# A one-core mixer and mixture-of-experts kernel: expert weights read in longer pieces, the scatter matmuls in one run, final_g by one transfer

## The chip, the cores and the metric

One Trainium2 chip, one of its cores. The time is device microseconds of one execution of the whole program; lower is better. A kernel's time is the median of several executions.

## The reference, cut to what matters

```python
def reference(x, ln1_g, ..., w_out, ln2_g, ..., w_exp_gate, w_exp_up, w_exp_down, final_g):
    ...
    for l in range(DEPTH):                                   # DEPTH = 1
        x = mixer_sublayer(x, ln1_g[l], w_in[l], ..., w_out[l])
        x = x + hier_moe(rmsnorm(x, ln2_g[l]), ...)
    return rmsnorm(x, final_g)

def hier_moe(h, w_rg, b_rg, w_re, b_re, w_gate, w_up, w_down):
    t = h.reshape(-1, d)                                     # 256 tokens x 1024
    ...                                                      # best group of 4, then its best 2 of 4 experts
    combine = jnp.sum(jax.nn.one_hot(expert_ids, N_EXPERTS, dtype=f32) * w_sel[..., None], axis=1)
    y = jnp.zeros((n, d), f32)
    for e in range(N_EXPERTS):                               # 16 experts, 512 channels inside
        a = jax.nn.silu(t @ w_gate[e]) * (t @ w_up[e])
        y = y + combine[:, e:e + 1] * (a @ w_down[e]).astype(f32)
    return ...
```

Everything is float32. The three expert weights hold 16 x 1024 x 512 numbers each, 2 MB per expert and matrix.

## The kernel before, in words

The program is one function. Its first part (up to 200 us) is the mixer: the projections of w_in, stick-breaking attention and the HGRN2 recurrence. Then come the projection by w_out with the routing, and the experts.

**What lies where.** x2 holds the 256 tokens as 2 tiles of 128 tokens (t = 0, 1) by 1024 channels. After the mixer it is split into xH (a copy rounded to the matmul's fp32r type, by ACT) and xL (the rest, by POOL), both in o_hl (lines 674 to 676), in plain channel order. A channel sits in the expert tiles at block k of 128 and partition p: channel 128k+p. The gain ln2_g is laid out to match by vectors() (line 266): a transpose of small rows into the columns `cols`, of which g2c is a part.

**Routing.** As each 256-channel quarter of w_out's product comes out of PE (o_mm), DVE adds it to x2 (o_add, line 668), ACT squares it for the norm (o_sq), PE transposes it (o_tr), DVE copies the transposes to SBUF (line 660) and PE multiplies them by the router weights (o_lg, line 664, into plg). route_rank (line 720) ranks the 20 logits by all-pair comparisons on DVE (ceq, cgt: lines 727 to 730); route_pos (line 736) numbers each expert's tokens with two small matmuls (prk) and makes posm; onehot (line 694) writes, for 4 experts and 64 rows each, the matrix Sr (in the buffer mr) that picks tokens. A function residual(i) adds a quarter of x to the output sum py[i] with two matmuls by the identity (line 830; moving operands xH and xL).

**Gather.** gather(q) collects for two pairs of experts the chosen tokens' rows, transposed: 32 matmuls with 128 channels of xH or xL as stationary operand and Sr as moving operand (line 928, tile pg; line 750 for the first), and ACT or DVE multiplies the result by g2c into xg.

**Expert pairs.** 16 experts are done as 8 pairs p = 0..7. For each pair PE does, in program order:

- gateup(p, "g"): 32 matmuls into pg (line 958), then gateup(p, "u"): 32 into pu. Each is 64 rows by 512 columns; the two experts j = 0, 1 of a pair alternate.
- scatter(p-1): 8 matmuls (line 992) add the previous pair's result yh to py. Four of them stand between the 16th and the 17th matmul of pu, four behind the 32nd.
- mid(p): ACT and DVE make silu(gate) times up in abuf, PE transposes it in 4 blocks (pT, line 967), DVE copies that to the buffer mf (line 968).
- for odd p the next gather; then prep(p+1): small matmuls into the tile pw (lines 943, 945), DVE copies two columns (cwall, lines 947, 948), ACT copies pw to STa in the buffer mr (line 949; listed in the trace as `ACT L60 mr<-pw`, since the helper at line 60 issues it).
- down(p): the columns in two halves, 16 matmuls into one PSUM tile pd and then 16 into the next (line 977); after each half weigh (line 981) scales it on ACT and DVE into yh.

The PSUM tiles pw, pT, pg of the gathers and pd share two tags, C0 and B0, in turn:

```python
911:     def wtile():
912:         wtile.n += 1
913:         return ("C0", "B0")[wtile.n % 2]
```

so a tile can be written only when the tile two places before it has been read out.

**Weights.** Every pair needs 12 tiles of 1 MB: gate and up of both experts in two halves of 512 channels, down in two column halves. SP issues their DMAs in the order of use, each as soon as one of a ring of 1 MB slots comes free. A transfer takes for each partition 4 rows that lie 128 rows apart in DRAM:

```python
880:                     wts[nm, p, j, kh] = load(
881:                         w[2 * p + j].rearrange("(k p) f -> p k f", p=P)[:, 4 * kh:4 * kh + 4], [4, DE],
```

that is 4 pieces of 2048 bytes (512 columns of 4 bytes). The last pair's down tiles are cut further.

**The end.** load_gain and bcast_gain (lines 997 to 1008) bring final_g as one row and spread it over 128 partitions with 4 matmuls (tile pgf) and two ACT copies, ahead of the last pair's pu. After the last pair's down the sum py is normalised and stored.

The order of PE's instructions is that of the program; a scheduler puts the other engines' instructions in order by readiness and priority, unless the code forces it.

Of the kernel before, what the change touches and what calls it, by code (L numbers as in the profile page):

```python
# [30 lines left out]
def hybrid_kernel(ctx: ExitStack, tc: tile.TileContext, x, ln1_g, w_in, w_bsb, w_bhg, hg_norm_g,  # L31
# [48 lines left out]
    rowt = blk("w0", [2, P], name="rowt")  # L80
# [4 lines left out]
    nc.scalar.dma_start(rows[12:20], ln2_g.rearrange("(k p) -> k p", p=P))  # L85

# [60 lines left out]
    cols = cp.tile([P, 20], F32, name="cols")  # L147
# [520 lines left out]
    def o_add(t, c0, c1, pp):  # L668
        V.tensor_add(x2[:, t, c0:c1], x2[:, t, c0:c1], pp)

    def o_sq(i, t, c0, c1):
        act(xL[:, t, c0:c1], x2[:, t, c0:c1], AF.Square, accum_out=ss2[:, t, i:i + 1])

    def o_hl(t, c0, c1):
        act(xH[:, t, c0:c1], x2[:, t, c0:c1], AF.Copy)
        nc.gpsimd.tensor_sub(xL[:, t, c0:c1], x2[:, t, c0:c1], xH[:, t, c0:c1].bitcast(F32))

    def o_ev(i, t, c0, c1, pp):
        o_add(t, c0, c1, pp)
        o_sq(i, t, c0, c1)  # L680
        o_hl(t, c0, c1)
# [38 lines left out]
    def route_rank(t):  # L720

        l5, c, e = lg[:, t], cgt[:, t], ceq[:, t]
        V.scalar_tensor_tensor(l5.rearrange("p g e -> p (g e)"), plg[:, t, 0:20], sc[:, t:t + 1], br,
                               ALU.mult, ALU.add)
# [11 lines left out]
    def route_pos(t):  # L736
# [8 lines left out]
        V.scalar_tensor_tensor(posm[:, t], prk[:, t], 1.0, self_[:, t], ALU.add, ALU.mult)  # L745

    def gather0(t):
        for k in range(KT):
# [28 lines left out]
    with tc.high_priority():  # L777
# [12 lines left out]
            (6, 3): [(o_lg, 2, 0), (o_tr, 3, 0)], (7, 0): [(o_lg, 3, 0), (route_rank, 0)],  # L790
            (7, 1): [(o_tr, 0, 1)], (7, 2): [(o_lg, 0, 1), (o_tr, 1, 1)], (7, 3): [(o_lg, 1, 1), (route_pos, 0)]}
    for n in (6, 7):
# [4 lines left out]
        if n == 6:  # L797
            o_ev(0, 1, 0, 512, pq[0, 1])
    mr = blk("yha", [4, 256], F32R, name="mr")
# [5 lines left out]
    with tc.high_priority():  # L805
        o_add(1, 512, 768, pq[1, 1][:, 0:256])
        o_sq(1, 1, 512, 768)
    o_tr(2, 1, "D1", late[0])
    with tc.high_priority():
        o_add(1, 768, 1024, pq[1, 1][:, 256:512])  # L810
        o_sq(2, 1, 768, 1024)
        V.tensor_add(ss2[:, 1, 0:1], ss2[:, 1, 0:1], ss2[:, 1, 1:2])
        route_pre(1)
    o_tr(3, 1, "B0", late[1])
    route_rms(1, 2, ss2[:, 1, 2:3])
    onehot(0, 0)
    o_hl(1, 512, 768)
    o_hl(1, 768, 1024)
    o_lg(2, 1, late[0])
    o_lg(3, 1, late[1])  # L820
    pgs = [ps.tile([P, 2, 256], F32, name="pg0_%d" % k2, tag=["A0", "A1", "C0", "B0"][k2]) for k2 in range(4)]
# [4 lines left out]
    def residual(i):  # L826
        t, dh = divmod(i, 2)
        py[i] = ps.tile([P, 512], F32, name="py_%d" % i, tag=PYT[i])
        for j, xx in enumerate((xH, xL)):
            nc.tensor.matmul(py[i], idr, xx[:, t, 512 * dh:512 * dh + 512],  # L830
                             start=j == 0, stop=False, skip_group_check=True)

    gather0(0)
    residual(0)
    route_rank(1)
    residual(1)
    route_pos(1)
    onehot(0, 1)
    residual(2)
# [45 lines left out]
    def load_d(p):  # L885
        for dh in range(2):
            src = [w_down[2 * p + j].rearrange("(k p) d -> p k d", p=P)[:, :, 512 * dh:512 * dh + 512]
                   for j in range(2)]
            cut = p == NP - 1
            for j in range(2):  # L890
                wts["d", p, j, dh] = load(src[j], [4, 512], parts=2 if cut else 1)
            if not cut:
                pieces = ()
            elif dh == 0:
                pieces = ((0, 2, 0, 512), (2, 4, 0, 512))
            else:
# [19 lines left out]
    def gather(q):  # L916
# [4 lines left out]
        for k2 in range(KT // 2):  # L921
# [10 lines left out]
            if k2 % 2:  # L932
                V.tensor_tensor(xg[:, ks], pg, g2c[:, ks, None].to_broadcast([P, 2, 256]), ALU.mult)
            else:
                for j in range(2):
                    k = 2 * k2 + j
                    act(xg[:, k], pg[:, j], AF.Copy, scale=g2c[:, k:k + 1])
# [13 lines left out]
    def gateup(p, nm, between=None):  # L951
        pt = ps.tile([P, DE], F32, name="p%s%d" % (nm, p), tag="A0" if nm == "g" else "A1")
        xg = xgs[p // 2][:, :, (p % 2) * P:(p % 2) * P + P]
        for k in range(KT):
            if k == KT // 2 and between:
                between()
# [5 lines left out]
    def mid(p, pgt, put):  # L962
# [3 lines left out]
        for f in range(4):  # L966
            nc.tensor.transpose(pT[:, f], abuf[:, f * P:f * P + P], ident)
        V.tensor_copy(aT_, pT)

    def down(p, c0, c1, between=None):  # L970
        pd = ps.tile([P, c1 - c0], F32, name="pd%d_%d" % (p, c0), tag=wtile())
        dh, o = c0 // 512, c0 // 512 * 512
        for f in range(4):
            if f == 2 and between:
                between()
            for j in range(2):
                nc.tensor.matmul(pd[j * 64:j * 64 + 64], aT_[:, f, j * 64:j * 64 + 64],  # L977
                                 wts["d", p, j, dh][:, f, c0 - o:c1 - o], start=f == 0, stop=f == 3)
        return pd

# [200 lines left out]
```

## Time and profile before

| | us |
|---|---|
| median of 3 runs | 459.32 (458.93 to 461.73) |
| the profiled execution's own time | 461.8 |
| its span on the core | 460.1 |
| PE busy in the span | 439.5 (96%) |
| mean granted TensorE clock in the span | 0.984 of full |

In the views PE is TensorE's matmuls, DVE VectorE, ACT ScalarE, POOL GpSimd, SP SyncE (it issues the DMAs). A tile's name is the program's, with numbers left out: wt a weight tile, pg, pu, pd and py the PSUM tiles above. "Idle before" is how long the engine stood still ahead of an instruction, with the engine that released it.

### The profile page before, as it was taken

The page shows a single profiled execution, that of the slowest core. Times are in us where ns is not written, and L with a number is a line of the kernel's source. Part 1 is how long each engine was busy: PE and PEld are TensorE (multiplying, and loading weights), DVE is VectorE, ACT ScalarE, POOL GpSimd, SP SyncE. Part 2 cuts the span into 40 slices and gives each one's busy share as a digit, 9 for nine tenths or more (in the row PEclk, how much of TensorE's full clock was granted, in tenths as well). Part 3 has the DMA queues.
Part 4 walks back from the last instruction along what each step waited for, and adds up shares of the span by engine and source line. Part 5 has one row for each costly group of instructions (what it writes and reads, how often), then busy time and mean ns, then how long its engine had stood idle before and what let it go on. Part 6 is the DMA issues. An engine that isn't in the chain of part 4 may idle for free.

```text
span 460.1 us, 6095 instructions
## 1 busy us (share of the span) xinstructions
PE 439.5 (96%) x2429; PEld 286.5 (62%) x2429; DVE 193.6 (42%) x315; ACT 149.4 (32%) x246; POOL 103.0 (22%) x121
## 2 busy tenths in 40 slices
PE   6999999999999999999998999999999999999991
PEld 6999899887777888878743345343633336343350
DVE  5878857595546647974722112020210203011032
ACT  6644335535656745523311102101110102101223
POOL 8464755675144200352200000000000000000000
PEclk9999999999999999999799999999999999999996
DMA  8945342525939999568959999999999999999952
GB/s 290 289 157 181 112 166 93 182 93 150 389 118 358 292 386 385 178 233 280 341 185 388 387 387 386 387 386 387 387 386 387 386 387 385 387 387 385 386 193 98
DMA packets 73852, 134.79 MB, mean 293 GB/s; under 512 B 2317, under 2 KB 14665, under 8 KB 73818
## 3 DMA queue, kind: packets, MB, share of 16 engines
q1 hardware_dynamic: 73634, 134.23, 81.7%
q8 instruction: 21, 0.34, 0.3%
q0 software_dynamic: 128, 0.09, 0.2%
q14 instruction: 13, 0.11, 0.1%
q10 hardware_dynamic: 56, 0.01, 0.0%
HBM read 133.28 MB, written 1.05 MB: 292 GB/s over the span
## 4 chain that ended last, share of the span: by engine, by line
PE 85%; DMA 4%; POOL 4%; DVE 2%; issue 2%; ACT 1%; POOLq 0%; ACTq 0%
PE pu L958 12%; PE pg L958 11%; PE pd L977 11%; PE pv L294 5%; PE pv L295 5%; PE pv L296 5%; PE py L992 4%; PE pp L200 3%; DMA wt<-in_w_exp_gate_dram 3%; PE pp L201 3%; PE pp L202 3%; PE pg L928 3%; PE pl L365 2%; PE pp L309 1%; PE pb L601 1%
## 5 line engine op out<-in xcount | busy, mean ns | idle before, releaser
L191 DVE TENSOR_TENSOR lp<-wt,hp 128x1024 fp32r<-128x1024 f32 (+1 forms) x43 | 59.6, 1405 | 23.0 <-ACT hp L60 22.6
L977 PE MATMUL pd<-wt,mf 128*64 128x512 f32 (+1 forms) x272 | 57.2, 571 | 2.6 <-ACT mr L60 1.4
L958 PE MATMUL pu<-wt,xg 128*64 128x512 f32 x256 | 58.6, 596 | 0.0
L958 PE MATMUL pg<-wt,xg 128*64 128x512 f32 x256 | 57.4, 593 | 0.5 <-DMA wt<-in_w_exp_gate_dram 0.5
L60 ACT ACTIVATE hp<-wt 128x1024 fp32r<-128x1024 f32 (+1 forms) x44 | 44.6, 1036 | 40.2 <-PE pp L201 26.7
L704 POOL TENSOR_SCALAR rb<-ss,rb 128x1 f32<-128x1 f32 x1 | 0.5, 527 | 226.2 <-ACT junk L60 226.2
L964 DVE SCALAR_TENSOR_TENSOR mf<-pu,cwall,mf 128x512 f32<-128x512 f32 x8 | 6.0, 752 | 106.1 <-PE pu L958 106.1
L958 PEld LDWEIGHTS pg<-wt,xg 128*64 128x64 f32 x256 | 18.9, 137 | 37.0 <-issue 35.2
L200 PE MATMUL pp<-hTH,hp 128*128 128x256 f32 x144 | 41.4, 287 | 0.0
L977 PEld LDWEIGHTS pd<-wt,mf 128*64 128x64 f32 x272 | 19.5, 137 | 34.9 <-issue 30.7
L201 PE MATMUL pp<-hTL,hp 128*128 128x256 f32 x144 | 40.7, 283 | 0.0
L202 PE MATMUL pp<-hTH,lp 128*128 128x256 f32 x144 | 40.7, 283 | 0.0
L958 PEld LDWEIGHTS pu<-wt,xg 128*64 128x64 f32 x256 | 18.6, 137 | 34.5 <-issue 33.3
L294 PE MATMUL pv<-hp,hTH 128*128 128x512 f32 x96 | 39.7, 414 | 0.0
L295 PE MATMUL pv<-lp,hTH 128*128 128x512 f32 x96 | 37.5, 391 | 0.0
L296 PE MATMUL pv<-hp,hTL 128*128 128x512 f32 x96 | 37.5, 391 | 0.0
L983 DVE SCALAR_TENSOR_TENSOR yh<-pd,cwall,yh 128x512 fp32r<-128x512 f32 (+1 forms) x16 | 11.7, 734 | 48.8 <-ACT yh L60 48.8
L60 ACT ACTIVATE yh<-pd,cwall 128x512 fp32r<-128x512 f32 (+1 forms) x16 | 10.8, 674 | 54.8 <-PE pd L977 54.8
L200 PEld LDWEIGHTS pp<-hTH,hp 128*128 128x128 f32 x144 | 27.6, 191 | 0.2
L201 PEld LDWEIGHTS pp<-hTL,hp 128*128 128x128 f32 x144 | 27.6, 192 | 0.0
L202 PEld LDWEIGHTS pp<-hTH,lp 128*128 128x128 f32 x144 | 27.6, 192 | 0.0
L294 PEld LDWEIGHTS pv<-hp,hTH 128*128 128x128 f32 x96 | 18.0, 188 | 5.0 <-issue 0.8
(277 smaller groups left out, 720.5 us busy)
## 6 DMA issues: line engine op xcount, KB each, us to landing
wt<-in_w_exp_gate_dram SPq DMA_DIRECT2D x32, 1024.0 KB, 13.7
wt<-in_w_exp_up_dram SPq DMA_DIRECT2D x32, 1024.0 KB, 13.9
wt<-in_w_exp_down_dram SPq DMA_DIRECT2D x28, 1024.0 KB, 14.1
wt<-in_w_in_dram SPq DMA_DIRECT2D x22, 1024.0 KB, 6.2
wt<-in_w_out_dram SPq DMA_DIRECT2D x4, 1024.0 KB, 7.1
wt<-in_w_exp_down_dram SPq DMA_DIRECT2D x6, 512.0 KB, 12.3
wt<-in_w_branch_sb_dram SPq DMA_DIRECT2D x2, 1024.0 KB
wt<-in_w_branch_hg_dram SPq DMA_DIRECT2D x2, 1024.0 KB, 6.4
```

Source lines behind the costliest of these rows:

```text
L60: i = nc.scalar.activation(out_, in_, func, **kw)
L191: low = (nc.gpsimd if i in pool else nc.vector).tensor_sub(l[:, sl], raw[:, sl], h[:, sl].bitcast(F32))
L200: nc.tensor.matmul(dst, ah, bh, start=i == 0, stop=False)
L201: nc.tensor.matmul(dst, ah, bl, start=False, stop=False)
L202: nc.tensor.matmul(dst, al, bh, start=False, stop=i == n - 1)
L294: nc.tensor.matmul(pp, hh, wh[:, k], start=kh == k == 0, stop=False)
L295: nc.tensor.matmul(pp, hh, wl[:, k], start=False, stop=False)
L296: nc.tensor.matmul(pp, hl, wh[:, k], start=False, stop=kh == 1 and k == 3)
L928: nc.tensor.matmul(pg[:, j], xx[:, t, k * P:k * P + P], Sr[:, t * 256:t * 256 + 256], start=i == 0, stop=i == 3)
L958: nc.tensor.matmul(pt[j * 64:j * 64 + 64], xg[:, k, j * 64:j * 64 + 64], wts[nm, p, j, k // 4][:, k % 4], start=k == 0, stop=k == KT - 1)
L977: nc.tensor.matmul(pd[j * 64:j * 64 + 64], aT_[:, f, j * 64:j * 64 + 64], wts["d", p, j, dh][:, f, c0 - o:c1 - o], start=f == 0, stop=f == 3)
L992: nc.tensor.matmul(total(t, c0, c1), STa[:, p % 2, t * P:t * P + P], yh[:, hl, c0:c1], start=False, stop=False, skip_group_check=True)
```

## The change

Five things change.

1. **Weights.** Each partition takes 4 rows (gate and up) or 2 rows (down) that lie side by side in DRAM: one piece of 8192 bytes. Down tiles are cut by the inner channel (fh) instead of by column half, with full rows; the last pair keeps column halves with short pieces, in 12 DMAs in place of 10.
2. **Channel order.** A tile's block and partition now mean channel 512kh+4p+r. xH and xL are stored in that order: o_h and o_l read x2 at every 4th number. residual reads xH and xL back at a stride of 128 numbers, the transposes of abuf take every second column, and vectors() makes a second gain g2p with 4 small transposes and one more load of ln2_g.
3. **Scatter** of the previous pair stands in one run of 8 matmuls behind pu. **Down** takes the inner channel as its outer loop, with both column halves open at once (down_rows).
4. **Order.** residual(2) and prep(1) move behind pair 0's pu and mid(0); DVE's order in the routing is forced, the first gather is split in two, and DVE instead of POOL does the last two pieces of xL.
5. **final_g** is spread by a transfer to 128 partitions; the row, the 4 matmuls and the 2 copies go.

```diff
-    rowt = blk("w0", [2, P], name="rowt")
+    rowt = blk("w0", [6, P], name="rowt")
...
+    row4 = rowt[:, 2:6].rearrange("p a b -> p (a b)")
+    nc.scalar.dma_start(row4[0:2], ln2_g.rearrange("(k c) -> k c", c=512))
...
+        for r in range(4):
+            nc.tensor.transpose(pcol[:, 20 + 2 * r:22 + 2 * r], row4[0:2, r::4], ident[:2, :2])
...
+    def rows4(xx, t, c0, c1):
+        k = c0 // 512 * 512
+        return xx[:, t, k:k + 512].rearrange("q (r p) -> q r p", r=4)[:, :, (c0 - k) // 4:(c1 - k) // 4]
+
+    def chan4(t, c0, c1):
+        return x2[:, t, c0:c1].rearrange("q (p r) -> q r p", r=4)
+
+    def o_h(t, c0, c1):
+        act(rows4(xH, t, c0, c1), chan4(t, c0, c1), AF.Copy)
+
+    def o_l(t, c0, c1, eng=nc.gpsimd):
+        eng.tensor_sub(rows4(xL, t, c0, c1), chan4(t, c0, c1), rows4(xH, t, c0, c1).bitcast(F32))
...
             nc.tensor.matmul(py[i], idr,
-                             xx[:, t, 512 * dh:512 * dh + 512],
+                             xx[:, t, 512 * dh:512 * dh + 512].rearrange("q (r p) -> q p r", r=4),
                              start=j == 0, stop=False, skip_group_check=True)
...
+    queue(add0, add1, marks["pos0"], oh, b0, b1, tr0, tr1)
+    gather0(0, range(0, 4))
...
+    gather0(0, range(4, KT))
+    route_rank(1)
     residual(0)
-    route_rank(1)
     residual(1)
     route_pos(1)
-    onehot(0, 1)
-    residual(2)
+    with tc.issue_after(onehot(0, 1)):
+        o_l(1, 512, 768, V)
+        o_l(1, 768, 1024, V)
     gather0(1)
...
-                        w[2 * p + j].rearrange("(k p) f -> p k f", p=P)[:, 4 * kh:4 * kh + 4], [4, DE],
+                        w[2 * p + j].rearrange("(k p r) f -> p k r f", p=P, r=4)[:, kh], [4, DE],
...
+        src = [w_down[2 * p + j].rearrange("(k p r) d -> p k r d", p=P, r=2) for j in range(2)]
+        if p < NP - 1:
+            for fh in range(2):
+                for j in range(2):
+                    wts["d", p, j, fh] = load(src[j][:, fh], [2, D])
+            return
...
-            nc.tensor.transpose(pT[:, f], abuf[:, f * P:f * P + P], ident)
+            nc.tensor.transpose(pT[:, f], abuf[:, f // 2 * 256 + f % 2:f // 2 * 256 + 256:2], ident)
...
+    def down_rows(p):
+
+        pds = [ps.tile([P, 512], F32, name="pd%d_%d" % (p, c), tag=wtile()) for c in range(2)]
+        for f in range(4):
+            for c in range(2):
+                for j in range(2):
+                    nc.tensor.matmul(pds[c][j * 64:j * 64 + 64], aT_[:, f, j * 64:j * 64 + 64],
+                                     wts["d", p, j, f // 2][:, f % 2, 512 * c:512 * c + 512],
+                                     start=f == 0, stop=f == 3)
+        return pds
...
-        nc.sync.dma_start(gf["g"][0:1, 1], final_g.unsqueeze(0))
-        gf["one"] = blk("m4", [P], name="onerow")
-        V.memset(gf["one"], 1.0)
-
-    def bcast_gain():
-        for dh in range(2):
-            ds = slice(dh * 512, dh * 512 + 512)
-            pg = ps.tile([P, 512], F32, name="pgf%d" % dh, tag=wtile())
-            nc.tensor.matmul(pg, gf["one"][0:1], gf["g"][0:1, 1, ds], start=True, stop=True)
-            act(gf["g"][:, 0, ds], pg, AF.Copy)
+        nc.sync.dma_start(gf["g"][:, 0], final_g.unsqueeze(0).to_broadcast([P, D]))
...
-        if p == NP - 1:
-            bcast_gain()
-        put = gateup(p, "u", (lambda: scatter(p - 1, yprev, 0, 512)) if p else None)
+        put = gateup(p, "u")
         if p:
+            scatter(p - 1, yprev, 0, 512)
             scatter(p - 1, yprev, 512, 1024)
         else:
+            residual(2)
             residual(3)
-            prep(1)
         mid(p, pgt, put)
...
-            if p:
-                prep(p + 1)
+            prep(p + 1)
         yprev = blk("x", [2, D], F32R, name="yh%d" % p)
         if p < NP - 1:
-            for c0 in (0, 512):
-                weigh(p, down(p, c0, c0 + 512), yprev, c0, c0 + 512)
+            for c, pd in enumerate(down_rows(p)):
+                weigh(p, pd, yprev, 512 * c, 512 * c + 512)
```

PE's instructions at the start of pair 1's down, before and after; wt are the weight tiles (two experts alternate), mf the transposed activations, and the brackets name the engines or DMA queues that a matmul waits for.

```order
L945 MATMUL pw_2367<-ident,mr 128x128 x2
L977 MATMUL pd_0_2377<-wt_2264,mf 64x512 [waits DMAHW0_49,DVE_49]
L977 MATMUL pd_0_2377<-wt_2266,mf 64x512 [waits DMAHW1_49]
...
L977 MATMUL pd_512_2388<-wt_2268,mf 64x512 [waits DMAHW2_49,Activation_49]
L977 MATMUL pd_512_2388<-wt_2270,mf 64x512 [waits DMAHW3_49]
```

```order
L984 MATMUL pw_2373<-ident,mr 128x128 x2
L1024 MATMUL pd_0_2383<-wt_2270,mf 64x512 [waits DMAHW0_49,DVE_49]
L1024 MATMUL pd_0_2383<-wt_2272,mf 64x512 [waits DMAHW2_49]
L1024 MATMUL pd_1_2384<-wt_2270,mf 64x512 [waits Activation_49]
L1024 MATMUL pd_1_2384<-wt_2272,mf 64x512
L1024 MATMUL pd_0_2383<-wt_2270,mf 64x512
L1024 MATMUL pd_0_2383<-wt_2272,mf 64x512
```

The first matmul into the second half, which waits for ACT, stood eight places behind the first one into the first half, and now stands two behind it.

PE's instructions in pair 1 between the last matmuls of pu and the transposes of mid(1); py are the output sums, yh the weighted result of pair 0.

```order
L958 MATMUL pu_2289<-wt_2256,xg_2131 64x512
L958 MATMUL pu_2289<-wt_2258,xg_2131 64x512
L992 MATMUL py_2070<-yh_2225,mr 128x512 [waits Activation_49]
L992 MATMUL py_2070<-yh_2225,mr 128x512 [waits DVE_49]
L992 MATMUL py_2088<-yh_2225,mr 128x512 x2
L958 MATMUL pu_2289<-wt_2260,xg_2131 64x512 [waits DMAHW4_49]
...
L992 MATMUL py_2081<-yh_2225,mr 128x512 [waits Activation_49]
L992 MATMUL py_2081<-yh_2225,mr 128x512 [waits DVE_49]
L992 MATMUL py_2205<-yh_2225,mr 128x512 x2
L967 MATMUL pT_2316<-ident,mf 128x128 [waits DVE_49]
```

```order
L995 MATMUL pu_2295<-wt_2268,xg_2134 64x512
L1040 MATMUL py_2082<-yh_2231,mr 128x512 [waits Activation_49]
L1040 MATMUL py_2082<-yh_2231,mr 128x512 [waits DVE_49]
L1040 MATMUL py_2208<-yh_2231,mr 128x512 x2
L1040 MATMUL py_2085<-yh_2231,mr 128x512 [waits Activation_49]
L1040 MATMUL py_2085<-yh_2231,mr 128x512 [waits DVE_49]
L1040 MATMUL py_2211<-yh_2231,mr 128x512 x2
L1004 MATMUL pT_2322<-ident,mf 128x128 [waits DVE_49]
```

The four py matmuls that stood inside pu moved behind it.

DVE's instructions in the routing, from the copy of the second token tile's transposes (xta) to the end of tile 0's ranking (lg, ceq, cgt, rank, og, sel); pq are the products of w_out.

```order
L660 COPY xta<-ptr_1974 128x256 [waits DVE_49,PE_49]
L723 SCALAR_TENSOR_TENSOR lg<-plg,sc_1804,br 128x20 [waits DMASW3_49,DMASW2_49,PE_49]
L727 TENSOR_TENSOR ceq<-lg 128x80 [waits DVE_49]
L728 TENSOR_TENSOR cgt<-lg 128x80
L729 TENSOR_TENSOR ceq<-ceq,ltri 128x80 [waits DVE_49]
L730 TENSOR_TENSOR cgt<-cgt,ceq 128x80 [waits DVE_49]
L660 COPY xta<-ptr_1998 128x256 [waits PE_49]
L731 TENSOR_REDUCE rank<-cgt 128x20 [waits DVE_49]
```

```order
L666 COPY xta<-ptr_1979 128x256 [waits DVE_49,PE_49]
L728 TENSOR_SCALAR sb_1810<-ss_1805 128x1 [waits Activation_49]
L729 TENSOR_SCALAR sb_1810<-sb_1810 128x1 [waits DVE_49]
L666 COPY xta<-ptr_1997 128x256 [waits PE_49]
L746 SCALAR_TENSOR_TENSOR lg<-plg,sc_1809,br 128x20 [waits DMASW3_49,DMASW2_49]
L750 TENSOR_TENSOR ceq<-lg 128x80 [waits DVE_49]
L751 TENSOR_TENSOR cgt<-lg 128x80
L752 TENSOR_TENSOR ceq<-ceq,ltri 128x80 [waits DVE_49]
```

The xta copy that stood behind the five comparisons of tile 0 now stands ahead of them.

## Rows read from the trace of the kernel before

**Rows 1.** The page: busy time of each engine; further down, GB/s in 40 slices of the span.

```profile
PE 439.5 (96%) x2429; PEld 286.5 (62%) x2429; DVE 193.6 (42%) x315; ACT 149.4 (32%) x246; POOL 103.0 (22%) x121
...
GB/s 290 289 157 181 112 166 93 182 93 150 389 118 358 292 386 385 178 233 280 341 185 388 387 387 386 387 386 387 387 386 387 386 387 385 387 387 385 386 193 98
```

**Rows 2.** Chain of waits, pair 1 and pair 7: start us, us, what (x matmuls).

```profile
258.68 6.87 PE pg L958 x32
265.55 3.43 PE pu L958 x16
268.98 1.12 PE py L992 x4
270.11 3.58 PE pu L958 x16
273.69 1.13 PE py L992 x4
274.83 0.46 PE pT L967 x4
...
408.04 14.48 DMA wt<-in_w_exp_gate_dram
...
422.57 3.65 PE pg L958 x14
426.21 1.91 PE pgf L1007 x4
...
432.83 4.23 PE pu L958 x16
```

**Rows 3.** Windows: us, busy of PE, PEld, DVE, ACT, POOL, granted clock, DMA share, GB/s.

```profile
340.00:360.00 20.00, 19.84 (x96) 7.65 (x94) 3.26 (x8) 1.76 (x3) 0.00 (x0) 1.00 1.05 387
...
234.00:235.00 1.00, 1.00 (x8) 0.34 (x6) 0.59 (x3) 0.03 (x1) 0.00 (x0) 1.00 0.00 0
...
4.00:5.00 1.00, 1.00 (x8) 1.00 (x6) 0.00 (x0) 0.26 (x1) 1.00 (x4) 1.00 1.00 403
...
12.00:14.00 2.00, 2.00 (x15) 1.75 (x14) 2.00 (x6) 2.00 (x5) 2.00 (x3) 1.00 1.06 335
```

**Rows 4.** Timeline of PE and ACT around down in pairs 0, 1 and 2.

```profile
251.60 0.65 PE L977 MATMUL pd<-wt,mf 128*64 128x512 f32 x2 [1.36 <-ACT mr L60]
...
280.19 1.51 PE L977 MATMUL pd<-wt,mf 128*64 128x512 f32 x6
...
280.90 0.38 ACT L60 ACTIVATE mr<-pw 128x256 fp32r<-128x256 f32 x1 [1.58 <-DVE cwall L948]
...
304.66 1.51 PE L977 MATMUL pd<-wt,mf 128*64 128x512 f32 x6 [0.17 <-DVE mf L968]
...
305.12 0.38 ACT L60 ACTIVATE mr<-pw 128x256 fp32r<-128x256 f32 x1 [10.22 <-DVE cwall L948]
```

**Rows 5.** Chain of waits: a run of 128x2 matmuls in the mixer.

```profile
40.86 1.70 PE pd L351 x16
```

**Rows 6.** Timeline of the routing, and a window in it (columns as in rows 3).

```profile
218.47 1.32 DVE L727 TENSOR_TENSOR ceq<-lg 128x80 f32<-128x80 f32 x1
...
220.75 0.62 PE L664 MATMUL plg<-wr,xta 128*128 128x20 f32 x4 [0.89 <-DVE xta L660]
...
223.87 1.90 PE L664 MATMUL plg<-wr,mf 128*128 128x20 f32 x8
...
229.58 0.60 PE L830 MATMUL py<-xL,tro 128*128 128x512 f32 x1
...
224.00:225.00 1.00, 1.00 (x6) 1.00 (x6) 1.00 (x3) 0.34 (x2) 0.89 (x2) 0.50 0.88 336
```

**Rows 7.** Timeline: residual's two matmuls; two copies, their targets in short and in long runs.

```profile
248.45 0.50 PE L830 MATMUL py<-xH,tro 128*128 128x512 f32 x1
248.79 0.40 PE L830 MATMUL py<-xL,tro 128*128 128x512 f32 x1
...
46.78 1.32 DVE L368 COPY_PREDICATED at<-cst,pl 128x512 f32<-128x512 int32 x1
...
62.85 0.71 DVE L368 COPY_PREDICATED at<-cst,pl 128x512 f32<-128x512 int32 x1 [0.34 <-PE pl L365]
```

More of the change, by code (lines that the diff above doesn't have):

```diff
@@ L744, in route_pos, with gather0 @@
             nc.tensor.matmul(prk[:, 1], trib, self_[:, 1], start=False, stop=True)
-        V.scalar_tensor_tensor(posm[:, t], prk[:, t], 1.0, self_[:, t], ALU.add, ALU.mult)
-    def gather0(t):
-        for k in range(KT):
+        marks["pos%d" % t] = V.scalar_tensor_tensor(posm[:, t], prk[:, t], 1.0, self_[:, t],
+                                                    ALU.add, ALU.mult).ins
+    def gather0(t, ks=range(KT)):
+        for k in ks:
             for i, xx in enumerate((xH, xL)):
@@ L804, in hybrid_kernel @@
     late = [mf[:, 2 + i].rearrange("p (a b) -> p a b", b=P) for i in range(2)]
[L805 to L821, printed above, removed]
+    pgs = [ps.tile([P, 2, 256], F32, name="pg0_%d" % k2, tag=["A0", "C0", "B0", "A1"][k2]) for k2 in range(4)]
     PYT = ["B1", "D1", "D0", "C1"]
@@ L829, in residual, with queue @@
         for j, xx in enumerate((xH, xL)):
-            nc.tensor.matmul(py[i], idr, xx[:, t, 512 * dh:512 * dh + 512],
+            nc.tensor.matmul(py[i], idr,
+                             xx[:, t, 512 * dh:512 * dh + 512].rearrange("q (r p) -> q p r", r=4),
                              start=j == 0, stop=False, skip_group_check=True)
-    gather0(0)
+    def queue(*ins):
+        for i0, i1 in zip(ins, ins[1:]):
+            nosync(i1, i0)
+    add0 = o_add(1, 512, 768, pq[1, 1][:, 0:256])
+    o_sq(1, 1, 512, 768)
+    o_tr(2, 1, "D1", late[0])
+    tr0 = marks["tr"]
+    add1 = o_add(1, 768, 1024, pq[1, 1][:, 256:512])
+    last_sq = o_sq(2, 1, 768, 1024)
+    o_tr(3, 1, "B1", late[1])
+    tr1 = marks["tr"]
+    oh = onehot(0, 0)
+    b0, b1 = rms_second(sb3[:, 1], ss2[:, 1, 1:2])
+    queue(add0, add1, marks["pos0"], oh, b0, b1, tr0, tr1)
+    gather0(0, range(0, 4))
+    with tc.issue_after(last_sq), tc.issue_after(tr1):
+        root = rms_last(sc[:, 1:2], ss2[:, 1, 2:3], sb3[:, 1])
+    with tc.issue_after(root):
+        o_h(1, 512, 768)
+        o_h(1, 768, 1024)
+    o_lg(2, 1, late[0])
+    o_lg(3, 1, late[1])
+    gather0(0, range(4, KT))
+    route_rank(1)
     residual(0)
-    route_rank(1)
     residual(1)
     route_pos(1)
-    onehot(0, 1)
-    residual(2)
+    with tc.issue_after(onehot(0, 1)):
+        o_l(1, 512, 768, V)
+        o_l(1, 768, 1024, V)
     gather0(1)
@@ L954, in gateup @@
         for k in range(KT):
-            if k == KT // 2 and between:
-                between()
             for j in range(2):
@@ L1098, in hybrid_kernel @@
         xs = blk("tH", [2, D], name="xs")
-        V.tensor_add(xs, xH.bitcast(F32), xL.bitcast(F32))
+        for t in range(2):
+            for k in (0, 512):
+                V.tensor_add(xs[:, t, k:k + 512].rearrange("q (p r) -> q r p", r=4),
+                             rows4(xH, t, k, k + 512).bitcast(F32), rows4(xL, t, k, k + 512).bitcast(F32))
         xd = blk("sh0", [2, D], name="xd")
```

60 lines of the change are left out of this document (31 added, 29 removed).

## The prediction

> **What bounds the kernel now.** I read the page first: PE is busy in 439.5 of 460.1 us [rows 1], so the end is set by PE, and the question is where it stands still and where its work can shrink. Next the chain of waits, pair by pair: a middle pair is a row of PE pieces without a gap (pg 6.87, two halves of pu 3.43 and 3.58 with 1.12 and 1.13 of py behind each, pT 0.46), and only the last pair has something else in it, a DMA wait before pg's last 14 matmuls [rows 2]. Then the windows and the page's GB/s: from about 241 us on, the transfers run without pause at 387 GB/s [rows 1, 3]. A 1.0486 MB tile therefore takes 2.71 us, a pair's 12 tiles take 32.5 us, and a middle pair's PE work is only a little less; the reserve of loaded tiles shrinks until PE catches up with the loads in pair 7. PE's own pace does not hang on the loads: it does 8 matmuls a microsecond with DMA at 0 GB/s and 96 in 20 us (many records are missing) with DMA at 387, busy all the time [rows 3]. Last the timeline around down, which shows when the ACT copy of pw ends against PE's work [rows 4].
>
> The sum is made for the profiled execution, whose span is 460.1 us and whose own time is 461.8, 0.5% over the median of 459.32; the difference is then taken to the median.
>
> **The change part by part.**
>
> *vectors().* Four more 128x2 transposes on PE. Sixteen matmuls of that size took 1.70 us [rows 5], 0.106 each, so +0.4. The added 4 KB load is hidden behind the w_in stage that comes before: 0.
>
> *Routing.* PE stood idle 0.89 us for the xta copy [rows 6], which stood behind tile 0's comparisons (one of them 1.32 us on DVE); the copy now goes ahead of them, so this wait goes. What is late next is tile 0's ranking, later by one or two copies, and with it the first onehot. Behind the wait the granted clock is 0.50 in 224 to 225 us [rows 6], the 1.2 GHz level; the work from 223.87 to 229.58+0.60 ran there, 6.3 us. If the clock stayed at 2.4 GHz, half of it, 3.1 us, could be won, if PE sets the pace there, though part of that stretch waits for DVE and ACT. With the clock as it was I count -0.2 (the 0.89 gone, most given back by the late onehot and by DVE's two pieces of xL), with the full clock -1.1. I take -0.5; ends +1 and -3.1.
>
> *Pair 0.* prep(1) and residual(2) come behind pu and mid(0). The wait of down(0) for ACT's copy of pw, 1.36 us [rows 4], shrinks since pd_1, not pd_0, needs it; residual(2) adds about 0.8, taken from the routing. -0.1.
>
> *Scatter in one run, pairs 1 to 6.* Before: 3.43+1.12+3.58+1.13 = 9.26 [rows 2]. After: pu without a break costs as much as pg, 6.87; eight py matmuls in a run cost 2.25 less the one change of shape that is saved. Where py and pu meet, a piece of pu is 0.15 longer (3.58 against 3.43); I count 2.04 for the eight. 8.91, so -0.37 a pair, -2.2 for six.
>
> *Down with both halves open.* pd_1 has the PSUM tag that pw had, so its first matmul waits for ACT's copy of pw. Before, 16 matmuls lay between the first of pd_0 and the first of pd_1; now two. In pair 1, pd started at 280.19 and ACT's copy ended at 280.90+0.38 = 281.28 [rows 4]. Two matmuls take 0.43 (7 us for 32). The stall is 281.28-280.19-0.43 = 0.66, with the semaphore about 0.7. In pair 2 the copy ended at 305.50, pd started at 304.66: 0.4, with the semaphore 0.5. Behind the stalled matmul stands everything on PE, since its queue is in order. Three odd pairs and three even ones: 2.1+1.5 = 3.6, and I take +3.5; ends 0 (if ACT comes earlier) and +5. While PE waits, nothing else covers it. weigh now comes after both halves, but py of the next pair is 64 matmuls away: 0.
>
> *The last pair.* pgf's 1.91 goes, with some 0.15 of changes of shape beside it. PE's waits for weights go, if the loads are early enough: pg(7) took 1.6 us more than 6.87 (it ended at 422.57+3.65 = 426.22, and had started at 417.75), and the second half of pu 4.23 against 3.58, 0.65 [rows 2]. The scatter gives 0.37. In all -1.91-0.15-1.6-0.65-0.37 = -4.7.
>
> *Loads.* What a piece of 8192 bytes does is not in this trace. The same queue did 335 GB/s from 12 to 14 us, in shorter pieces, 387 with pieces of 2048 bytes, and 403 from 4 to 5 us, with x's pieces of 4096 bytes in it [rows 3]. An estimate carried on from these is 413, or 2.54 us a tile; the ends are 403 or more (2.60) and, for a loss, 375, 3% under the row of today. What PE needs: the last tile of up(7) landed at 432.83+0.6 = 433.4, and 240.75+71x2.71 gives just that, so about 71 tiles came one behind the other. In the new kernel PE needs it at 432.83-1.91-0.15-1.6-1.12-0.15+1.5 = 429.4 (without pgf, the wait in pg and the py between the halves of pu, and 1.5 later by the terms of the earlier stages), and final_g's 512 KB, half a tile, come before it: 240.75+1.3+71t must not pass 429.4, so t must be at most 2.64, 397 GB/s. Over that each 0.01 us costs 0.7. At 413 GB/s there is room and the loads leave the path.
>
> The Trainium skill speaks against this ("DMA: Bandwidth & Descriptors", section "Where 436 GB/s comes from"): for transfers from HBM to SBUF the HBM side binds at about 358 GB/s, whatever the pieces. This trace shows 387 over 20 us [rows 3], so the figure does not hold here; if a limit of that kind stood at today's rate, the case would be rival B.
>
> *Strides.* xH and xL are read and written at steps of 16 and 512 bytes. residual's two matmuls start 0.34 apart [rows 7]; the eight make 2.7. A copy by mask took 1.32 us into short runs and 0.71 into long ones [rows 7], a factor of 1.86. If it held for residual, +2.3, and for the four 128x256 pieces on ACT and DVE at 0.38 [rows 4], +1.3, in all 3.6; if pT's blocks paid it as well, 8x0.46x0.86 = 3.2 more. If nothing pays, 0. I take +0.4, near the low end, since in most of the stretch the engine is not the one waited for, and the mask copy is a different operation.
>
> The Trainium skill ("Advanced Engine Details and Errata", section "SBUF Cachelines") says that SBUF lines are 16 bytes and that a different line with each access is slower. By it the strides would cost, which is rival C; the mask copies of [rows 7] lean that way, and no row shows a matmul so.
>
> Sum: +0.4-0.5-0.1-2.2+3.5-4.7+0.4 = -3.2. So 458.6 of 461.8 for the profiled execution, and 456.1 against the median.
>
> **The rivals.**
>
> A. *The wait of pd_1 does not arise, or the full clock comes to the routing.* For it: the scheduler of ACT and DVE is free, and prep's copies may come earlier; the low clock began after an idle PE. Against it: the order shows the wait. -3.5 and -0.6 more of the routing: -3.2-4.1 = -7.3, 452.0. Chance 0.17.
>
> B. *The loads are no faster with long pieces.* For it: a flat 387 in all the stretch looks like a ceiling. Against it: shorter pieces are slower, 4096 bytes are faster. t = 2.71: 71x0.07 = 5.0 over the threshold, 5.0-3.2 = +1.8: 461.1. Chance 0.10.
>
> C. *Strided reads pay.* For it and against it as above; 3.6 in place of 0.4: -3.2+3.2 = 0, 459.3. Chance 0.11.
>
> D. *Slower: pieces of 8192 bytes load slower.* A partition's whole 8 KB comes as one piece, so fewer pieces are under way at once. In place of 71 tiles at 2.71, 71 at 2.80 (375 GB/s): 71x0.16 = 11.4 over the threshold, -3.2: +8.2, 467.5. It decides from t = 2.64+3.2/71 = 2.69 (390 GB/s) on, above which the new kernel isn't faster. Against it: rate rose with the piece in each row. Chance 0.06.
>
> **How the numbers follow.** The forecast, 456.1, has 0.56, its own range 453.5 to 458.5. The low end, 451.5, is A with 0.5 to spare; the high end, 461.5, takes in B and C and leaves out D. 1% is 4.6 us, about what a measurement of this kernel tells from no change: faster is under 454.7, slower over 463.9. Of the forecast's 0.56 some 0.2 lies under 454.7, with A's 0.17 that makes 0.37. Slower is D and a little of B, 0.07. The rest, 0.56, is within 1%.
>
> **What would show it.** Windows between 260 and 400 us: DMA near 413 GB/s while it runs, with pauses. Timeline: pd in pieces of 2 and 30 matmuls with 0.4 to 0.8 us idle behind ACT mr in pairs 1 to 6; pu of 32 matmuls in 6.9 us and py of 8 in about 2.0. In the last pair no idle time behind a DMA. If DMA waits stand before pg in pairs 3 to 7, D or B is right; if residual's matmuls start over 0.5 apart, C is. If pd shows no wait, A. I am wrong as a whole if a stage before 200 us moves by more than 1 us, since nothing there should.

## The result and the profile after

The changed kernel takes 456.28 us (median of 6 runs, 455.52 to 457.36), the kernel before 459.32: a ratio of 0.9915, with a 95% interval of 0.989 to 0.9941, that is 3.0 us or 0.8% less. The forecast was 456.1, within 1%. The profiled execution of the changed kernel has a span of 455.6 us, 4.5 less than the one of before; at 457.36 it is the slowest of the changed kernel's six.

The page of the changed kernel, against [rows 1]: busy time by engine, and GB/s in 40 slices.

```profile
PE 434.5 (95%) x2429; PEld 285.5 (63%) x2429; DVE 194.3 (43%) x317; ACT 150.1 (33%) x244; POOL 102.1 (22%) x119
...
GB/s 286 238 179 182 135 117 162 93 96 190 292 238 270 309 325 411 278 132 372 292 227 414 388 426 421 421 421 423 421 420 424 418 421 423 420 313 229 401 155 99
```

The loads run at 421 GB/s where they stood at 387, and near the end there is a hole (229) that was not there before.

Chain of waits of the changed kernel, pair 1, the start of pair 2's down, and pair 7, against [rows 2].

```profile
258.66 6.87 PE pg L995 x32
265.53 6.87 PE pu L995 x32
272.39 2.06 PE py L1040 x8
274.45 0.47 PE pT L1004 x4
...
280.54 0.39 ACT mr L60
280.93 0.04 issue
280.98 6.23 PE pd L1024 x28
...
304.25 7.13 PE pd L1024 x32
...
416.62 6.87 PE pg L995 x32
423.49 7.86 PE pu L995 x32
431.35 2.05 PE py L1040 x8
```

pu and py are what the prediction said (6.87 and 2.05). ACT's copy of pw stands in the chain of pair 1, since pd_1 waits for it; in pair 2, down runs through. pg of the last pair waits for nothing, but its pu takes 7.86 in place of 6.87. The timeline has down of pairs 1 and 2 as a whole:

```profile
279.82 7.39 PE L1024 MATMUL pd<-wt,mf 128*64 128x512 f32 x32
...
304.25 7.13 PE L1024 MATMUL pd<-wt,mf 128*64 128x512 f32 x32 [0.17 <-DVE mf L1005]
```

Windows of the changed kernel, against [rows 3, 6].

```profile
9.00:10.00 1.00, 0.94 (x5) 0.94 (x6) 0.82 (x5) 0.95 (x2) 0.23 (x1) 0.50 1.09 359
15.00:16.00 1.00, 1.00 (x7) 1.00 (x7) 1.00 (x4) 1.00 (x3) 1.00 (x2) 0.59 0.00 0
340.00:360.00 20.00, 19.84 (x98) 7.94 (x96) 3.82 (x9) 1.67 (x3) 0.00 (x0) 1.00 1.02 422
407.00:413.00 6.00, 5.83 (x32) 3.00 (x32) 1.14 (x5) 0.38 (x1) 0.00 (x0) 1.00 0.08 33
```

The clock is at its lower level, 1.2 GHz, from 9 to almost 16 us, where the kernel before had 2.4; and from 407 to 413 us the loads stand still, with PE at full work.

Two stages that no term of the prediction spoke of have thus moved: the start, and the last pair's up weights. Here are the waits of PE in the first 20 us, of the changed kernel and then of the kernel before (us in total, times, longest):

```profile
PE pt L241 <- DVE v_n L160: 2.0, 1, 2.0
PE warm L142 <- POOL ident masks.py:199: 1.8, 1, 1.8
PE pt L241 <- DVE xn L235: 0.6, 1, 0.6
```

```profile
PE warm L140 <- POOL ident masks.py:199: 1.8, 1, 1.8
PE pt L239 <- DVE v_n L158: 1.2, 1, 1.2
PE pt L239 <- DVE xn L233: 0.5, 1, 0.5
```

ACT's order there, of the kernel before and then of the changed kernel. xn at 6.36 and 6.04 is the square of the second token tile; y_n at 5.92 and 7.10 is the Ln of the first tile's norm, with the second tile's behind it in the changed kernel:

```profile
5.92 0.29 ACT L60 ACTIVATE y_n<-ss,epst 128x1 f32<-128x1 f32 x1
...
6.36 1.04 ACT L60 ACTIVATE xn<-x 128x1024 f32<-128x1024 f32 x1
```

```profile
6.04 1.06 ACT L60 ACTIVATE xn<-x 128x1024 f32<-128x1024 f32 x1
...
7.10 0.47 ACT L60 ACTIVATE y_n<-ss,epst 128x1 f32<-128x1 f32 x2
```

In the trace of the changed kernel DVE's second scaling of x is slow as well, 1.86 us where the kernel before took 0.75:

```profile
9.73 1.86 DVE L235 TENSOR_SCALAR xn<-x,ss 128x1024 f32<-128x1024 f32 x1
```

The table shows where the time went, by when stages begin in the traces. The second column takes, from a later trace of the kernel before (span 457.9), the same stages with the full clock in the routing; the first trace had it at 0.50 there. The last column adds up to the difference of the spans, 455.6 against 457.9.

| stage | before, first trace | before, later trace | after | after less later trace |
|---|---|---|---|---|
| start, to the first pp of w_in's main loop | 17.57 | 17.68 | 20.94 | +3.3 |
| mixer, to w_out's first product | 176.1 | 176.1 | 176.1 | 0 |
| w_out and routing, to pg of pair 0 | 40.0 | 37.3 | 37.0 | -0.2 |
| pair 0, to pg of pair 1 | 24.9 | 24.9 | 24.4 | -0.5 |
| pairs 1 to 6 | 159.1 | 159.1 | 158.0 | -1.1 |
| pair 7, to its last pd | 30.8 | 30.7 | 27.0 | -3.7 |
| from there to the end | 11.8 | 12.2 | 12.2 | 0 |

### The profile page after: what moved, and what is told of

Same layout as the page of the kernel before. It is cut to its first block, busy times and chain, and to the rows that moved or that the text cites. A ratio compares the mean times of both kernels' runs of the same rounds, so it can differ in the third digit from the quotient of the medians.

```text
span 455.6 us, 6088 instructions
## 1 busy us (share of the span) xinstructions
PE 434.5 (95%) x2429; PEld 285.5 (63%) x2429; DVE 194.3 (43%) x317; ACT 150.1 (33%) x244; POOL 102.1 (22%) x119
## 4 chain that ended last, share of the span: by engine, by line
PE 87%; POOL 4%; DVE 3%; issue 2%; ACT 1%; DMA 1%; SPq 0%; POOLq 0%; ACTq 0%; DVEq 0%
PE pu L995 12%; PE pg L995 12%; PE pd L1024 10%; PE pv L300 5%; PE pv L302 5%; PE pv L301 5%; PE py L1040 4%; PE pp L202 3%; PE pp L204 3%; PE pp L203 3%; PE pg L966 3%; PE pl L371 2%; PE pd L1014 2%; PE pp L315 1%; PE pb L608 1%
## 5 line engine op out<-in xcount | busy, mean ns | idle before, releaser
L995 PE MATMUL pu<-wt,xg 128*64 128x512 f32 x256 | 57.3, 593 | 0.0
L995 PE MATMUL pg<-wt,xg 128*64 128x512 f32 x256 | 56.3, 592 | 0.0
L1024 PE MATMUL pd<-wt,mf 128*64 128x512 f32 x224 | 50.4, 598 | 0.9 <-DVE mf L1005 0.7
L1024 PEld LDWEIGHTS pd<-wt,mf 128*64 128x64 f32 x224 | 14.8, 136 | 31.7 <-issue 24.0
L1031 DVE SCALAR_TENSOR_TENSOR yh<-pd,cwall,yh 128x512 fp32r<-128x512 f32 (+1 forms) x16 | 11.7, 734 | 50.8 <-ACT yh L60 50.5
```

The lines of the kernel that those rows point to most:

```text
L995: nc.tensor.matmul(pt[j * 64:j * 64 + 64], xg[:, k, j * 64:j * 64 + 64], wts[nm, p, j, k // 4][:, k % 4], start=k == 0, stop=k == KT - 1)
L1024: nc.tensor.matmul(pds[c][j * 64:j * 64 + 64], aT_[:, f, j * 64:j * 64 + 64], wts["d", p, j, f // 2][:, f % 2, 512 * c:512 * c + 512], sta ...
```

## The experiments

Times are medians; the kernel before ran beside each group and had 459.65, 460.19 and 459.57 in the three groups, so the ratio to it is given with each. "The changed kernel" has 0.9915 (0.989 to 0.9941).

**1. The weights in short pieces again** (a_short): the layout of weights and channels of before, everything else of the change kept.

```diff
-                        w[2 * p + j].rearrange("(k p r) f -> p k r f", p=P, r=4)[:, kh], [4, DE],
+                        w[2 * p + j].rearrange("(k p) f -> p k f", p=P)[:, 4 * kh:4 * kh + 4], [4, DE],
...
-        src = [w_down[2 * p + j].rearrange("(k p r) d -> p k r d", p=P, r=2) for j in range(2)]
+        src = [w_down[2 * p + j].rearrange("(k r p) d -> p k r d", p=P, r=2) for j in range(2)]
```

Expected: 

> The changed kernel with the weights as before in plain channel order: gate and up in pieces of 2048 bytes, down in pieces of 4096, no strided reads, all other edits kept. Theory (the longer pieces raise the rate from 387 to 421 GB/s, and that pays): DMA at 387 to 400 GB/s without a pause, PE waits for weights in the last pair or two; up(7)'s last tile is needed at about 427 and lands at 431 to 434.5, so 3 to 6.6 more: 459.3 to 462.9. Rival (the loads were hidden anyway, and the gain is all in PE's order): 456.3, or a little less without the strided reads.

Measured: 459.81 us, ratio 1.000 (0.998 to 1.002). Window, and waits of PE from 400 to 440 us:

```profile
340.00:360.00 20.00, 19.84 (x98) 7.83 (x95) 2.64 (x8) 1.07 (x2) 0.00 (x0) 1.00 1.04 388
```

```profile
PE pu L995 <- DMA wt<-in_w_exp_up_dram: 3.5, 3, 1.6
```

The loads are back at 388 GB/s in this window (394 from 260 to 400 us; down's pieces have 4096 bytes), and PE waits 3.5 us for the last up weights. Without the long pieces the kernel is 3.5 us slower than the changed kernel, by medians, and the other edits together give nothing. No run has the long pieces alone. The kernel before waited 1.6 and 0.65 us for weights in its last pair [rows 2], so by an estimate they could have given it some 2.3; the rest of the 3.5 needs the other edits.

**2. Only the scatter in one run, in the kernel before** (b_scatter).

```diff
-        put = gateup(p, "u", (lambda: scatter(p - 1, yprev, 0, 512)) if p else None)
+        put = gateup(p, "u")
         if p:
+            scatter(p - 1, yprev, 0, 512)
```

Expected: 

> The kernel before with the scatter's eight matmuls in one run behind pu, nothing else. Theory (PE saves 0.3 to 0.37 in each of seven pairs, but the last pair waits for weights that come at a rate of their own, so that all but the last pair's share is given back there): pu and py together 8.9 instead of 9.26 in pairs 1 to 6, the wait ahead of pg's second half in pair 7 longer by about 2, the whole 0 to 0.5 less: 458.8 to 459.6. Rival (the sum as the prediction made it, every pair's gain counted): 2.6 less, 456.9.

Measured: 461.66 us, ratio 1.0028 (1.0008 to 1.0048). Waits of PE from 400 to 440 us:

```profile
PE pg L958 <- DMA wt<-in_w_exp_gate_dram: 2.5, 2, 1.6
PE pu L958 <- DMA wt<-in_w_exp_up_dram: 0.8, 1, 0.8
```

PE reaches the last pair earlier: the interval from pg of pair 1 to pg of pair 7 is 156.8 in place of 159.1. All of that is given back as waits for weights, and a little more, where I had expected 0 to 0.5 less. The four py that filled the time ahead of up(7)'s last tile now stand behind it. So the rate of the loads bounded the kernel before, and a PE edit alone can't be added to a sum.

**3. final_g's load behind the last pair's weights** (a_gain).

```diff
-            if p == NP - 1 and nm == "u":
-                load_gain()
...
         load_d(p)
+        if p == NP - 1:
+            load_gain()
```

Expected: 

> The changed kernel with final_g's load issued behind the last pair's weights, not ahead of up(7). Theory: SP stands at that load from 390.4 to 413.2 us until its slot comes free, all of up(7) is queued behind it, and pu of the last pair takes 7.86 instead of 6.87 for it; with the load behind, the transfers don't pause at 407 to 413 us, pu takes 6.87, the whole 1.0 less: 455.3. Rival (the slots of the ring, not the queue, are what up(7) waits for): pause and pu as they were, 456.3. Rival 2 (final_g now comes too late for the last products): over 456.3.

The wait that the theory rests on, in the view of the DMA queue's own waits, 385 to 430 us, of the changed kernel:

```profile
SPq L1047 <- PE pd L1024: 20.7, 1, 20.7
```

Measured: 455.28 us, ratio 0.9912 (0.9892 to 0.9933). Times alone don't separate it from the changed kernel; the trace does. Window and chain of this kernel:

```profile
410.00:412.00 2.00, 2.00 (x12) 0.67 (x10) 0.00 (x0) 0.00 (x0) 0.00 (x0) 1.00 1.02 426
```

```profile
421.71 6.87 PE pu L993 x32
```

The hole in the loads is closed and pu is down to 6.87. SP stood 20.7 us at final_g's load in the changed kernel. Its buffer has the slot of pair 6's first down tile, and everything that SP had behind this load, all of up(7), waited with it although its own slots were free. The change did not bring this wait in: in the kernel before, final_g's row stood at the same place and waited for a slot of pair 6's down as well, but only 3.7 us, and the loads ran on at 387 GB/s from 407 to 413 us. SP reached that place at 410.6 us there, and at 392.5 in the changed kernel.

```profile
SPq L999 <- PE pd L977: 3.7, 1, 3.7
```

**4. Down in two column halves** (a_halves).

```diff
-        for f in range(4):
-            for c in range(2):
+        for c in range(2):
+            for f in range(4):
```

Expected: 

> The changed kernel with down in two column halves one behind the other, the tiles as they are. Theory (a matmul in float32 leaves two records, so pd_0's first two matmuls take 0.9 us, and the stall of pd_1 is only 0.25 to 0.3 in pairs 1, 3 and 5 and nothing in the even ones): pd in pair 1 takes 7.1 instead of 7.39, the whole 0.8 less: 455.5. Rival (the stall as the prediction had it, 0.7 and 0.5, in part hidden from the chain): 3.5 less, 452.8. Rival 2 (another tile is late in the other order): no gain or a loss.

Measured: 456.46 us, ratio 0.9935 (0.9918 to 0.9952): no gain. The interval from pu of pair 1 to pg of pair 2 is 21.38 in place of 21.68, so the stall of 0.30 was there and is gone. But the last pair lost more (waits of PE, 400 to 440 us):

```profile
PE pu L995 <- DMA wt<-in_w_exp_up_dram: 1.7, 2, 1.3
```

In halves, pair 6's first down tile is in use until three quarters of down are done instead of half; final_g's load waits for that tile's slot, and up(7) behind it. The second rival came true, by the mechanism of experiment 3.

**5. ACT's order at the start as before** (a_start). The diff, cut to its main lines, adds an edge on ACT, from the first tile's Exp to the second tile's square (sq1 is that square):

```diff
+            if t:
+                nosync(sq1, marks["y_n10"])
```

Expected: 

> The changed kernel with ACT's order at the start as it was before: the square of the second token tile behind the two small steps of the first tile's norm. Theory 1 (the loss at the start comes from that order): DVE's first xn comes at 7.0 us instead of 8.25, PE's idle time before its first transposes falls from 2.0 to about 1.2 us, the granted clock stays at 1.00 between 9 and 15 us, the first pp of line 202 comes at about 18.1 instead of 20.94, and the whole takes 453.5 (-2.8). Rival (the clock only falls elsewhere: the routing of the kernel before ran at 0.50, and here it will again): the start is faster by 2.9 us, the routing slower by about 2, and the whole is within 0.8 of 456.3. Rival 2 (the later start comes from the added load of ln2_g): no change at the start.

Measured: 454.45 us, ratio 0.9887 (0.987 to 0.9905). Window and timeline:

```profile
10.00:15.00 5.00, 4.56 (x31) 3.85 (x30) 4.45 (x10) 5.00 (x11) 5.00 (x6) 1.00 0.87 273
```

```profile
18.18 0.39 PE L202 MATMUL pp<-hTH,hp 128*128 128x256 f32 x1
```

The clock stays up and pp comes at 18.18, as expected; the routing keeps the full clock, so the rival falls. By medians the gain is 1.8, not 2.8, and by the ratios 1.3; the intervals of the two ratios overlap, so the times alone don't settle its size. The trace of the changed kernel had the low clock in its whole start. In four other traces with the same ACT order (experiments 1, 3, 4 and 8) pp comes at 20.12, 19.12, 19.02 and 19.41. In the two of them with the full clock and DVE's second xn at 0.75 it comes at 19.12 and 19.02, so the old order is worth 0.8 to 0.9 there. In experiment 1 the clock was full as well, but that xn took 1.78 us.

**6. The changed kernel's ACT order in the kernel before** (b_late): the edge the other way round, from the second square to the first tile's Ln.

Expected: 

> The kernel before with ACT's order at the start as the changed kernel has it: both squares ahead of the first norm's small steps, and no added load or transposes. Theory (that order alone costs what the changed kernel lost at its start): the first xn comes at 8.25 instead of 7.04 us, PE waits about 2.0 us ahead of its first transposes, and the whole takes 1 to 2.5 more: about 461.4. Rival (the added load of ln2_g and the four transposes were the cause, or the weights' rate absorbs the delay before the end): within 0.5 of the kernel before.

Measured: 460.30 us, ratio 1.0017 (0.9996 to 1.0038). Waits of PE in the first 20 us:

```profile
PE pt L241 <- DVE v_n L158: 1.1, 1, 1.1
PE pt L241 <- DVE xn L235: 0.4, 1, 0.4
```

pp came at 18.76 in place of 17.57 to 17.68, 1.1 later, and the clock stayed up in this execution. So the order alone costs about 1.1 at the start, less than I expected. The total can't be told from no change with this interval, and the part of the rival by which the weights' rate absorbs the delay is not excluded. The added load and transposes are not needed for the shift at the start.

**7. A second trace of the kernel before** (b_again).

Expected: 

> The kernel before, unchanged, for a second trace. If the routing of this execution has the full clock, it takes about 9.4 to 10.4 us from w_out's last product to the first pg of pair 0, against 11.7 in the first trace, and the changed kernel's 9.7 is mostly the clock's doing. If it takes 11.7 again with the clock at 0.50, the low clock belongs to the old order of the routing.

Measured: one run of 459.61 us. Windows of this trace and of the first one:

```profile
224.00:230.00 6.00, 5.76 (x41) 4.96 (x42) 4.70 (x28) 2.79 (x7) 1.72 (x2) 1.00 0.90 299
```

```profile
224.00:230.00 6.00, 6.00 (x26) 5.82 (x27) 4.23 (x22) 2.36 (x6) 1.67 (x2) 0.50 0.89 316
```

With the old order the routing can have the full clock: 9.0 us from the last product of w_out to pg of pair 0, against 11.7 with the low clock. The wait of 0.9 for xta is in both [rows 6], so the clock differs between executions of one program.

**8. final_g by matmuls in the changed kernel** (a_pgf): the lines that the change took out are put back.

Expected: 

> The changed kernel with final_g spread by four matmuls as before. Theory (the matmuls cost 1.9 of PE, but up(7), which is late by 1.0 behind final_g's load in the queue, gets that much time): pgf 1.9 in the chain, pu 6.87 instead of 7.86, the whole 0.9 more: 457.2. Rival (all of the 2.06 that the prediction took comes back): 458.3.

Measured: 457.15 us, ratio 0.9944 (0.9925 to 0.9962), as the theory had it. Chain of waits:

```profile
421.92 1.91 PE pgf L1055 x4
423.83 7.02 PE pu L995 x32
```

pgf takes 1.91 and pu is shorter by 0.84. The transfer thus saves 1.9 us of matmuls, and 0.8 of it is lost again, since PE then reaches up(7) earlier and up(7) is late in both kernels: here SP stands 19.8 us at final_g's load, although it brings a single row.

**9. Both repairs** (a_sg), and **10. both repairs and down in halves** (a_best).

Expected of a_sg: 

> The changed kernel with both repairs: ACT's order at the start as before, and final_g's load behind the last pair's weights. Theory (the two losses are apart in place and mechanism, 1.8 and 1.0): 453.4, with pp of line 202 at 18.2 us and pu of the last pair 6.87. Rival (PE comes earlier by 2.9 us, so that the weights become the bound again): DMA waits before pg or pu of the last pairs, and over 454.

Expected of a_best: 

> As a_sg, and down in two column halves, one behind the other. Theory (with final_g's load out of the way the halves lose nothing in the last pair, and pd_1's stall of 0.25 goes in pairs 1, 3 and 5): 0.75 below a_sg, 452.7; no DMA wait in the last pair. Rival (the halves hold the weight slots longer, so that up(7) is late by that, as it was with final_g in front): pu of the last pair over 7.5 and the same as a_sg or more.

Measured: 454.03 us, ratio 0.9871 (0.9847 to 0.9896), and 453.45 us, ratio 0.9853 (0.9829 to 0.9876). Chain of waits of a_best, down of pair 6 and pair 7:

```profile
405.71 7.09 PE pd L1024 x32
412.80 6.87 PE pg L995 x32
419.66 6.87 PE pu L995 x32
426.53 2.06 PE py L1040 x8
```

In both no DMA wait is left in the last pair, so the rivals fall. The start of a_sg's trace is not what was expected: with the old order on ACT its pp comes at 20.09, not 18.2, and the median is 0.6 over the 453.4 expected.

```profile
10.00:15.00 5.00, 3.35 (x17) 3.04 (x16) 4.08 (x10) 4.63 (x11) 3.92 (x5) 0.72 0.89 284
```

ACT and DVE waited there for the first weight tile of w_in until 10.37 us (9.17 in experiment 5), PE for ACT, and then the clock was at its lower level from 13 to 15 us. In a_best, with the same start, the clock stays up and pp comes at 18.08. The old order thus does not keep every execution from a late start.

a_best takes 26.0 us from pg of pair 7 to its last pd, where the changed kernel takes 27.0 and the kernel before 30.8. The intervals of a_sg and a_best overlap, so the gain of the halves (0.6 by medians, 0.75 expected) isn't settled by times. By the traces pairs 1 to 6 take 157.0 in place of 158.0, and pair 7 takes 26.0 in both. a_best is the fastest kernel here, 1.5% under the kernel before and clear of the changed kernel by its interval.

## Why the prediction was right, point by point

The time came out within 0.2 us of the forecast. Part of that is luck: two terms were wrong by 2 to 3 us each in the trace, with opposite signs.

- **Loads: right.** 413 GB/s were estimated, 421 came (2.49 us a tile in place of 2.54). D and B fall: B's price was 5.0 over the forecast, and putting the short pieces back (with down in 4096-byte pieces) costs 3.5. The prediction quoted the Trainium skill ("DMA: Bandwidth & Descriptors", section "Where 436 GB/s comes from") with its limit of about 358 GB/s on the HBM side, which that section works out as half of 716 GB/s, for two cores. The trace shows 421 with one core at work, so the figure was no bound here, and no run has a second core.
- **Scatter: right.** 2.06 for eight py, 2.04 predicted; pu and py 8.93 instead of 9.26 in a pair, 0.33 less. The prediction's own 9.26 - 8.91 is 0.35 and not 0.37, and its 2.25 less one change of shape of 0.15 would be 2.10 and not 2.04; both slips are small. Experiment 2 adds the condition under which it counts: the loads must have room.
- **pd_1's stall: right in mechanism, wrong in size.** "Two matmuls take 0.43" failed. The trace shows 32 entries for both halves, where the order shows eight matmuls a half: a float32 matmul leaves two entries. (The kernel's description gives entries too: pg and pu are 16 matmuls each, and down has 8 a half. So 8 matmuls lay between the first of pd_0 and the first of pd_1, not 16.) The two matmuls ahead of pd_1 are thus four entries, 0.9 us. Down takes 7.39 in pair 1 and 7.13 in pair 2, so the stall is 0.26 in pair 1 and nothing shows in pair 2; experiment 4 has 0.30. The term +3.5 was about +0.9, and the stage of pairs 1 to 6 came to -1.1, where the prediction had +1.3. Rival A's first half, that the wait does not arise, came true for the greater part.
- **The start: missed.** The prediction had 0.4 there and called a shift of over 1 us before 200 us the sign that it is wrong as a whole. The measured +3.3 has three pieces. The four transposes took 0.5, as counted (experiment 5 against the kernel before, 18.18 against 17.68). The order on ACT is the second: the diff does not touch these lines, but both squares stand ahead of the first Ln in the changed kernel, and I had read the order in the routing and the expert pairs only. Experiments 5 and 6 put it at 0.8 to 1.1 in traces with the full clock. The rest, some 1.7 to 1.9 us, is DVE's slow second xn (1.1 longer; experiment 1 has it at the full clock, with pp at 20.12) and the low clock of this execution. It is not the order's doing alone: other traces with the same order are without it, and a_sg has a late start with the old one.
- **Last pair: right up to the queue.** -4.7 predicted, -3.7 measured, -4.7 with final_g's load out of the way (26.0 against 30.7). The step that failed is "final_g's 512 KB, half a tile": I counted its bytes, not that it waits for a slot at the head of a queue. The bytes are not what costs: in experiment 8 a single row waits 19.8 us there.
- **Routing: small, as the prediction had it, but the weighing was off.** -0.5 was taken, between -0.2 with the low clock and -1.1 with the full one. Two traces at full clock show -0.2 (37.0 against 37.3): the 0.9 of waiting for xta is gone and most of it is given back later, as was said. Against the first trace it is -2.9, near the end of -3.1 that the prediction kept for the clock, which comes and goes.
- **Pair 0: small, and a little better.** -0.5 measured, -0.1 predicted: the wait of 1.36 for ACT's copy of pw is gone altogether.
- **Strides: right in the sum.** Rival C fell: 0.4 was taken. With the plain order (experiment 1) the stage of w_out and routing is 0.14 shorter (36.90 against 37.04), pair 0 0.16 and pairs 1 to 6 0.25, in all 0.55. The prediction's price for residual started from 0.34 [rows 7], which has a change of shape in it; within a run residual's matmuls start 0.24 apart in plain order and 0.27 with strides. But the engines paid: ACT's copy to xH took 1.09 us in place of 0.61 for 128x512. The Trainium skill ("Advanced Engine Details and Errata", section "SBUF Cachelines") expects a price for touching a new 16-byte line each time; this trace agrees. Here it cost little: PE's waits from 205 to 240 us are the same four with either order (0.8, 0.6, 0.6 and 0.4 us), none of them for xH or xL.

What stays open: why the clock falls in one execution and not in another, and why DVE's second xn takes 0.75 us in most traces and 1.8 in two. No run here changed either alone.

## What to carry to other kernels

When a load queue has been the bound, first give it room and then count the matmuls saved: the scatter in one run was worth nothing before, and its 0.33 us a pair came out after. A small load at the head of an in-order queue holds up everything behind it until its own slot is free: here 20.7 us on the queue, of which 1.0 reached PE. Put it last unless it is needed first. And compare the order listing of every engine from the first row, since a scheduler can move lines that the diff doesn't touch.

## What I had not expected of the hardware

- Reading 8192 bytes at a stretch, the DMA engines moved 422 GB/s over 20 us, against 387 for 2048 bytes; 413 was predicted.
- Reading or writing SBUF at a step of 16 bytes in float32 slowed the engines unequally. The summary of the tiles xH and xL in the changed kernel, 210 to 236 us (ns, least, median, most), and then the same with the plain order (experiment 1):

```profile
L60 ACT ACTIVATE xH<-x x5: 639/1091/1109, 214.0 to 228.0; 128x512 fp32r<-128x512 f32 x3, 128x256 fp32r<-128x256 f32 x2
...
L692 POOL TENSOR_TENSOR xL<-x,xH x3: 1527/1537/1550, 215.1 to 222.3; 128x512 fp32r<-128x512 f32 x3
...
L692 DVE TENSOR_TENSOR xL<-x,xH x2: 602/604/606, 231.7 to 232.2; 128x256 fp32r<-128x256 f32 x2
```

```profile
L60 ACT ACTIVATE xH<-x x5: 401/612/615, 213.2 to 227.0; 128x512 fp32r<-128x512 f32 x3, 128x256 fp32r<-128x256 f32 x2
...
L692 POOL TENSOR_TENSOR xL<-x,xH x3: 1283/1284/1288, 213.9 to 221.0; 128x512 fp32r<-128x512 f32 x3
...
L692 DVE TENSOR_TENSOR xL<-x,xH x2: 417/418/418, 230.8 to 231.1; 128x256 fp32r<-128x256 f32 x2
```

ACT pays a factor of 1.78, DVE 1.45 and POOL 1.20. residual's matmuls, which read at a step of 512 bytes, start 0.27 apart in place of 0.24.
